# A decoder step on one core: every engine's order made by playing the program through with instruction durations

## The chip, the core and the metric

The kernel runs on one core of a Trainium2 chip, as one launch. The metric is the device time of that launch in microseconds; a lower time is better. A core has five engines that run side by side: TensorE (PE, matrix products), VectorE (DVE), ScalarE (ACT), GpSimd (POOL) and SyncE (SP, which here issues the DMAs). Each takes its instructions in the order in which the built program lists them, and a semaphore makes an instruction wait for what it needs from another engine.

## The reference

Two layers of a decoder trunk: an mLSTM mixer and a gated delta-net mixer, each followed by a squared-ReLU MLP, with a layer norm after every part. One sequence of 512 tokens starts from zero state, and eight sequences of 4 new tokens continue from stored states. D_MODEL is 1024, D_FF 4096; all is float32.

```python
def trunk(x, C, n, m, S, conv, ...):
    for layer in range(2):
        if layer % 2 == 0:
            y, Cj, nj, mj = mlstm_mixer(x, ...)        # 8 heads, key width 64, value width 128
        else:
            y, Sj, cj = gdn_mixer(x, ...)              # 16 value heads, 8 key heads, width 128
        x = layer_norm(ALPHA * x + y, ...)
        x = layer_norm(ALPHA * x + square(relu(x @ w1)) @ w2, ...)

def gated_delta_chunked(q, k, v, g, beta, S0):
    ...
    M = where(strict, (kb @ kc.T) * decay, 0)          # within a chunk
    A = M + eye(L)
    u, w = triangular_solve(A, [vc * beta, kb * exp(G)])
    attn = (qc @ kc.T) * decay
    def step(S, xc):                                   # from chunk to chunk
        v_new = u_c - w_c @ S
        o = qg_c @ S + attn_c @ v_new
        S = gL_c * S + kdec_c.T @ v_new
        return S, o
```

## The kernel before

All 544 tokens (512 of the prompt, 32 of the samples) lie side by side along the free dimension, in two halves of 272 columns; the features lie on the partitions in 8 blocks of 128. A projection's weight block is loaded by DMA (`wraw`, 512 KB), split into a high and a low part on ACT (L111) and DVE (L112), and multiplied in three products for each of 8 blocks and each half (`mm3`, L194). Such a 128 x 272 matmul of line 194 is the bulk of PE's work; the text calls it W. Both layers' MLPs are W almost alone.

The delta-net stage works in 8 units of two value heads (u = 0 to 7). The written order is a list:

```python
ORDER = "p0 p1 p2 p3 y0 w0 p4 p5 y1 w1 p6 p7 y2 w2 y3 w3"
PERIODS = {"p0": (3, 3, 4), "y0": (5, 5, 6), "p7": (3, 3, 6)}
```

`p` is the projections of a unit with the convolution (`conv`), `y` the output gate of a pair of units (`gate_out`), `w` the output projection. Each of them is 192 W. The small work runs in three lanes beside them, as generators that stop at each `yield`. After each group of three W, `mm3` calls `tick()`; a lane whose period is up then writes its next step into the program. `finish(...)` writes the rest of the named steps at once, as `gate_out` needs for the scans and the decode of its pair.

- Lane i, `prepare` and `invert`: products of the keys (L1093), decays (L1099, L1102), then a substitution of 15 steps on DVE (L1128, L1130) with DMAs through DRAM on both sides (`dg`, `ub`, `dx`, `xc`), then the inversion of eight triangular blocks in six groups of small matmuls: L1167 and L1174 (blocks of 32 x 16), L1188 and L1196/L1199 (32 x 32), L1208 and L1214 (64 x 64). Between two groups ACT or DVE copies the result.
- Lane s, `scan`: over 4 chunks of 128 tokens; in each chunk the products with the state (L1257), the solve with the inverse (L1268), the update of the state (L1275), the output (L1284), the head norm on ACT and DVE, and the transpose of the output (L1246, called the turn), which stands ahead of the next chunk's L1257.
- Lane d, `decode` and `update`: the sample tokens of a pair of units (L1315 to L1400), and their state updates (L1422) with loads and stores of `sst`.

The mLSTM stage has a list of its own (`ORDER_A`), with chunks of its scan on L742, L743, L757, L759, L762, and the transpose L735; its decode ends in L821, L824 and L834. Its scans and decodes are written with a raised priority (`high_priority(offset=HP)`), the loads of weights with `AHEAD`. A layer norm sums squares on PE (L356, L370) and sums on L367 and centres on L341.

All engines' final orders are made by the tile scheduler when `TileContext` is left: it takes the instructions by priority (the order in which they are written, less an offset) as their inputs and buffers come free. Buffers limit how far W can run ahead of the lanes: `kq` has 3 (`NKQ`), the PSUM tags have 3, 2, 2 and 1 (`BANKS`).

## Time and profile before

| what | us |
|---|---|
| median of 3 runs | 1823.6 |
| lowest, highest | 1813.73, 1825.53 |
| profiled execution, device time | 1814.86 |
| its span, first to last instruction | 1813.2 |
| PE busy | 1742.2 |
| DVE busy | 1062.3 |
| ACT busy | 831.2 |

The profiled execution lies near the lowest run. Busy times are unions over an engine's instructions. A PE row lasts until its modelled end, and rows overlap, so a step's cost on PE is read from the starts of rows that follow each other. The granted clock is 1.00 at PE's full 2.4 GHz and 0.50 at 1.2 GHz; in a window it is the mean.

### The profile page before, as it was taken

The page shows a single profiled execution, that of the slowest core. Times are in us where ns is not written, and L with a number is a line of the kernel's source. Part 1 is how long each engine was busy: PE and PEld are TensorE (multiplying, and loading weights), DVE is VectorE, ACT ScalarE, POOL GpSimd, SP SyncE. Part 2 cuts the span into 40 slices and gives each one's busy share as a digit, 9 for nine tenths or more (in the row PEclk, how much of TensorE's full clock was granted, in tenths as well). Part 3 has the DMA queues.
Part 4 walks back from the last instruction along what each step waited for, and adds up shares of the span by engine and source line. Part 5 has one row for each costly group of instructions (what it writes and reads, how often), then busy time and mean ns, then how long its engine had stood idle before and what let it go on. Part 6 is the DMA issues. An engine that isn't in the chain of part 4 may idle for free.

```text
span 1813.2 us, 35720 instructions
## 1 busy us (share of the span) xinstructions
PE 1742.2 (96%) x14580; PEld 1678.0 (93%) x14580; DVE 1062.3 (59%) x2648; ACT 831.2 (46%) x1874; POOL 56.1 (3%) x105
## 2 busy tenths in 40 slices
PE   7999999999999999899979999999898999999997
PEld 7999998999999999899869989998898999999996
DVE  6564767432244368777856877785488543234436
ACT  6444346331244137775644764575246542134314
POOL 2000000000000000011001000000000000000000
PEclk9999999999999999899979999997799999999998
DMA  4131232222223221223324323421242222222311
GB/s 161 59 106 62 70 97 93 71 94 82 94 82 117 82 75 62 56 58 102 104 64 143 105 66 104 141 80 39 78 132 73 94 85 91 90 86 93 106 59 50
DMA packets 84293, 158.89 MB, mean 88 GB/s; under 512 B 37536, under 2 KB 41504, under 8 KB 83616
## 3 DMA queue, kind: packets, MB, share of 16 engines
q1 hardware_dynamic: 84128, 156.60, 27.6%
q8 instruction: 115, 1.88, 0.4%
q14 instruction: 50, 0.41, 0.1%
HBM read 140.51 MB, written 16.06 MB: 86 GB/s over the span
## 4 chain that ended last, share of the span: by engine, by line
PE 80%; DVE 10%; ACT 4%; DMA 3%; issue 1%; POOL 1%; SPq 0%; ACTq 0%; DVEq 0%; POOLq 0%
PE pg_t L194 39%; PE pm_s L194 13%; PE pm_a L194 12%; PE pm_s L1371 2%; DVE lnt L380 1%; PE pm_s L1422 1%; DVE lnt L381 1%; PE pm_s L1257 1%; DMA xc<-dx 1%; PE pm_s L1268 1%; PE pm_a L1093 1%; DVE wl L112 1%; DVE acc L998 1%; PE pm_s L1275 1%; DVE XL L392 1%
## 5 line engine op out<-in xcount | busy, mean ns | idle before, releaser
L112 DVE TENSOR_TENSOR wl<-wraw,wh 128x1024 fp32r<-128x1024 f32 x200 | 245.3, 1227 | 370.6 <-ACT wh L111 369.8
L194 PE MATMUL pg_t<-XH,wh 128*128 128x272 f32 x1480 | 443.9, 300 | 3.3 <-ACT wh L111 2.8
L194 PE MATMUL pg_t<-XH,wl 128*128 128x272 f32 x1480 | 437.6, 296 | 1.0 <-DVE wl L112 1.0
L194 PE MATMUL pg_t<-XL,wh 128*128 128x272 f32 x1480 | 438.3, 296 | 0.0
L111 ACT CAST wh<-wraw 128x1024 fp32r<-128x1024 f32 (+1 forms) x201 | 210.1, 1045 | 472.7 <-PE pg_t L194 221.2
L194 PEld LDWEIGHTS pg_t<-XH,wh 128*128 128x128 f32 x1480 | 284.6, 192 | 7.4 <-ACT wh L111 4.5
L194 PEld LDWEIGHTS pg_t<-XH,wl 128*128 128x128 f32 x1480 | 283.8, 192 | 3.1 <-DVE wl L112 1.7
L194 PEld LDWEIGHTS pg_t<-XL,wh 128*128 128x128 f32 x1480 | 284.4, 192 | 2.0
L194 PE MATMUL pg_t<-h,wh 128*128 128x272 f32 x672 | 129.2, 289 | 0.0
L194 PEld LDWEIGHTS pg_t<-h,wh 128*128 128x128 f32 x672 | 105.8, 189 | 0.3
L194 PE MATMUL pg_t<-h,wl 128*128 128x272 f32 x336 | 97.0, 289 | 0.0
L194 PE MATMUL pm_a<-h,wh 128*128 128x272 f32 x496 | 95.3, 289 | 0.0
L194 PE MATMUL pm_s<-h,wh 128*128 128x272 f32 x496 | 95.0, 289 | 0.0
L194 PE MATMUL pm_s<-XH,wh 128*128 128x272 f32 x288 | 84.7, 294 | 0.0
L194 PE MATMUL pm_s<-XL,wh 128*128 128x272 f32 x288 | 84.4, 293 | 0.0
L194 PE MATMUL pm_s<-XH,wl 128*128 128x272 f32 x288 | 84.3, 293 | 0.0
L194 PE MATMUL pm_a<-XL,wh 128*128 128x272 f32 x280 | 82.3, 294 | 0.8 <-DVE XL L392 0.8
L396 DVE SCALAR_TENSOR_TENSOR XR<-XR,pg_t 128x272 f32<-128x272 f32 x118 | 51.0, 434 | 54.4 <-PE pg_t L194 53.9
L194 PE MATMUL pm_a<-XH,wh 128*128 128x272 f32 x280 | 82.6, 295 | 0.0
L194 PE MATMUL pm_a<-XH,wl 128*128 128x272 f32 x280 | 81.3, 290 | 0.0
L194 PEld LDWEIGHTS pm_s<-h,wh 128*128 128x128 f32 x496 | 78.0, 189 | 0.2
L194 PEld LDWEIGHTS pm_a<-h,wh 128*128 128x128 f32 x496 | 78.0, 188 | 0.1
(573 smaller groups left out, 3910.8 us busy)
## 6 DMA issues: line engine op xcount, KB each, us to landing
wraw<-in_w SPq DMA_DIRECT2D x64, 512.0 KB, 3.5
wraw<-in_wb SPq DMA_DIRECT2D x48, 512.0 KB, 3.5
wraw<-in_w2a SPq DMA_DIRECT2D x32, 512.0 KB, 3.5
sst<-in_s SPq DMA_DIRECT2D x64, 256.0 KB, 3.1
wraw<-in_wa SPq DMA_DIRECT2D x24, 512.0 KB, 3.5
wraw<-in_w2b SPq DMA_DIRECT2D x24, 512.0 KB, 3.5
wraw<-in_wbo SPq DMA_DIRECT2D x16, 512.0 KB, 3.7
out_ss<-sst SPq DMA_DIRECT2D x32, 256.0 KB, 2.7
```

Of the source, the lines that this page charges most:

```text
L111: S.copy(hi, src)
L112: V.tensor_tensor(lo, src, r32(hi), op=ALU.subtract)
L194: T.matmul(ps, lhsT=wt[:, k, :], rhs=xt[k][:, HS[h]], start=first and k == 0 and q == 0, stop=last and k == n - 1 and q == 2,)
L380: V.tensor_tensor(t, x, rs, op=ALU.mult)
L381: V.tensor_tensor(t, t, mu, op=ALU.subtract)
L392: V.tensor_tensor(XL[j][:, HS[h]], x, r32(XH[j][:, HS[h]]), op=ALU.subtract)
L396: V.scalar_tensor_tensor(x, x, ALPHA if first else 1.0, ps, op0=ALU.mult, op1=ALU.add)
L998: V.scalar_tensor_tensor(acc, pre[:, q:q + WC], cw[q], acc, op0=ALU.mult, op1=ALU.add)
L1093: T.matmul(pk[:, q * 256:(q + 1) * 256], lhsT=kq[:, 0, c0:c0 + P], rhs=kq[:, :, c0:c0 + P], start=True, stop=True)
L1257: T.matmul(pks[:, w], lhsT=kq[:, w, cc], rhs=St, start=True, stop=True)
L1268: T.matmul(pv[:, j], lhsT=X[:, 4 * (ch // 2) + 2 * j + ch % 2], rhs=rhs[:, j] if ch else vtok[:, j, 0], start=True, stop=True)
L1371: T.matmul(pkq[:, r], lhsT=t[:, r], rhs=kqf[:, :, o:o + 4], start=True, stop=True)
```

## The change

One keyword is given to the tile context. The scheduler then makes the orders by playing the program through with a duration for every instruction, from its own table, and gives an engine the next instruction at the time at which that play has it free. The kernel's functions, lists, buffers and priorities stay as they are.

```diff
-    with tile.TileContext(nc) as tc:
+    with tile.TileContext(nc, schedule_with_timeline_sim=True) as tc:
         hybrid_kernel(tc, *args)
```

Every engine's order changes: PE's by 9453 lines of difference, DVE's by 3606, ACT's, SP's and POOL's too. The number of instructions of each kind is the same on each engine. Three places on PE, before and after. In the names `pg_t`, `pm_a`, `pm_s` and `pm_t` are PSUM tiles, XH and XL the split activations, wh and wl the split weights.

The inversion of unit 0, lane i, at its fifth group, L1208, and the sixth, L1214. Before, 7 W stand between the two:

```order
L194 MATMUL pg_t<-XL_89,wh 128x272
L1208 MATMUL pm_a<-ZX,U 64x64 x8
L194 MATMUL pg_t<-XH_81,wl 128x272
L194 MATMUL pg_t<-XH_82,wh 128x272
L194 MATMUL pg_t<-XL_90,wh 128x272
L194 MATMUL pg_t<-XH_82,wl 128x272
L194 MATMUL pg_t<-XH_75,wh 128x272
L194 MATMUL pg_t<-XL_83,wh 128x272
L194 MATMUL pg_t<-XH_75,wl 128x272
L1214 MATMUL pm_a<-X,ZX 64x64 x8
```

After, the same place in PE's order; 25 W stand between L1208 and L1214, of which the first nine are shown:

```order
L194 MATMUL pg_t<-XL_83,wh 128x272
L194 MATMUL pg_t<-XH_75,wl 128x272
L1208 MATMUL pm_a<-ZX,U 64x64 x8
L194 MATMUL pg_t<-XH_76,wh 128x272
L194 MATMUL pg_t<-XL_84,wh 128x272
L194 MATMUL pg_t<-XH_76,wl 128x272
L194 MATMUL pg_t<-XH_77,wh 128x272
L194 MATMUL pg_t<-XL_85,wh 128x272
L194 MATMUL pg_t<-XH_77,wl 128x272
L194 MATMUL pg_t<-XH_78,wh 128x272
L194 MATMUL pg_t<-XL_86,wh 128x272
L194 MATMUL pg_t<-XH_78,wl 128x272
```

What moved: more W lie between two groups, and the whole inversion lies later against the W's, from the 5129th W to the 5163rd before and from the 5199th to the 5332nd after.

The scan of unit 0, lane s, from the turn (L1246) ahead of its second chunk, with steps of unit 1's preparation (L1093, L1099, L1102) and of the decode (L1315) between. Before:

```order
L1246 MATMUL pm_s<-ident,go_on 128x128 x2
L1257 MATMUL pm_s<-St,kq 128x256 x2
L1093 MATMUL pm_a<-kq 128x256
L1099 LDWEIGHTS identb
L1099 MATMUL pm_a<-maskw,identb 128x512
L1102 MATMUL pm_a<-RRb,hmr 128x256 x2
L194 MATMUL pg_t<-XL_83,wh 128x272
L194 MATMUL pg_t<-XH_75,wl 128x272
L194 MATMUL pg_t<-XH_76,wh 128x272
L194 MATMUL pg_t<-XL_84,wh 128x272
L194 MATMUL pg_t<-XH_76,wl 128x272
L1268 MATMUL pm_s<-rhs,X 128x128
```

After, the same steps:

```order
L1246 MATMUL pm_s<-ident,go_on 128x128 x2
L1257 MATMUL pm_s<-St,kq 128x256 x2
L1099 LDWEIGHTS identb
L1099 MATMUL pm_a<-maskw,identb 128x512
L1102 MATMUL pm_a<-RRb,hmr 128x256 x2
L1268 MATMUL pm_s<-rhs,X 128x128 x2
L1275 MATMUL pm_s<-vd,ktok 128x256
L1315 MATMUL pm_s<-blk,exprow 128x4
L1284 MATMUL pm_s<-vn,A 128x128 x2
L1323 MATMUL pm_s<-onesr,kqs 128x1 x2
L1246 MATMUL pm_s<-ident,go_on 128x128 x2
L1257 MATMUL pm_s<-St,kq 128x256 x2
```

What moved: W's no longer stand between the steps of a chunk; the next one comes after the L1268 of the fourth chunk.

The scan of unit 1, at the same point of its third chunk, with decode (L1400) and state updates (L1422) between. Before:

```order
L1246 MATMUL pm_s<-ident,go_on 128x128 x2
L1257 MATMUL pm_s<-St,kq 128x256 x2
L1400 MATMUL pm_s<-ident,onx 128x128
L1268 MATMUL pm_s<-rhs,X 128x128 x2
L1422 MATMUL pm_s<-VM,KM 128x512 x3
L194 MATMUL pg_t<-XH_75,wh 128x272
L1275 MATMUL pm_s<-vd,ktok 128x256
L194 MATMUL pg_t<-XL_83,wh 128x272
L194 MATMUL pg_t<-XH_75,wl 128x272
L194 MATMUL pg_t<-XH_76,wh 128x272
L194 MATMUL pg_t<-XL_84,wh 128x272
L194 MATMUL pg_t<-XH_76,wl 128x272
```

After, where the W's are those of the output projection (gyh is the gated output):

```order
L1246 MATMUL pm_s<-ident,go_on 128x128 x2
L1257 MATMUL pm_s<-St,kq 128x256 x2
L1400 MATMUL pm_s<-ident,onx 128x128
L1268 MATMUL pm_s<-rhs,X 128x128 x2
L1422 MATMUL pm_s<-VM,KM 128x512 x3
L194 MATMUL pg_t<-gyh,wh 128x272 x3
L1275 MATMUL pm_s<-vd,ktok 128x256
L1284 MATMUL pm_s<-vn,A 128x128 x2
L1422 MATMUL pm_s<-VM,KM 128x512 x3
L1246 MATMUL pm_s<-ident,go_on 128x128 x2
L1257 MATMUL pm_s<-St,kq 128x256 x2
L1422 MATMUL pm_s<-VM,KM 128x512 x3
```

What moved: the gate projection's W (XH, XL) stand ahead of this scan, and the scan runs into the inversion of unit 2 with three W in all.

## Rows read from the trace of the kernel before

**Rows 1.** The page's first part: span and PE's busy time
```profile
span 1813.2 us, 35720 instructions
...
PE 1742.2 (96%) x14580; PEld 1678.0 (93%) x14580; DVE 1062.3 (59%) x2648; ACT 831.2 (46%) x1874; POOL 56.1 (3%) x105
```

**Rows 2.** Busy time by stretches: PE, PEld, DVE, ACT, POOL, granted clock, DMA
```profile
50.00:250.00 200.00, 198.44 (x1543) 190.24 (x1542) 113.02 (x327) 87.02 (x274) 0.22 (x2) 1.00 0.24 78
250.00:320.00 70.00, 66.20 (x456) 61.34 (x455) 52.15 (x114) 43.27 (x82) 0.00 (x0) 0.95 0.29 91
350.00:650.00 300.00, 300.00 (x2389) 299.63 (x2388) 113.99 (x144) 85.41 (x123) 0.00 (x0) 1.00 0.28 90
650.00:1400.00 750.00, 709.36 (x6564) 666.09 (x6563) 553.51 (x1664) 433.28 (x1095) 43.27 (x74) 0.94 0.30 88
900.00:950.00 50.00, 40.42 (x425) 35.47 (x424) 28.23 (x93) 20.30 (x59) 3.54 (x8) 0.77 0.25 68
```

**Rows 3.** The chain that ended last, one piece in the first MLP
```profile
402.60 3.02 PE pg_t L194 x24
```

**Rows 4.** PE's timeline, inversion of unit 0, W left out: start, length, instruction
```profile
782.52 0.73 PE L1167 MATMUL pm_a<-DT,U 32*32 32x16 f32 x64 [0.76 <-DVE cvo L991]
...
784.40 0.73 PE L1174 MATMUL pm_a<-DB,Z 32*32 32x16 f32 x64
...
786.57 0.69 PE L1188 MATMUL pm_a<-DT,U 32*32 32x32 f32 x32
...
790.08 1.14 PE L1208 MATMUL pm_a<-ZX,U 64*64 64x64 f32 x16
...
792.22 1.14 PE L1214 MATMUL pm_a<-X,ZX 64*64 64x64 f32 x16
```

**Rows 5.** W alone in two stretches: PE, PEld, granted clock, DMA
```profile
782.50:793.50 11.00, 6.13 (x34) 4.62 (x34) 1.00 0.18 55
911.90:923.80 11.90, 0.82 (x2) 0.50 (x2) 0.50 0.16 56
```

**Rows 6.** PE's timeline, inversion of unit 2, first and last group
```profile
911.99 1.05 PE L1167 MATMUL pm_a<-DT,U 32*32 32x16 f32 x64 [4.31 <-DVE DT L1159]
...
921.80 1.97 PE L1214 MATMUL pm_a<-X,ZX 64*64 64x64 f32 x16 [0.68 <-ACT ZX L1210]
```

**Rows 7.** PE's timeline, two waiting steps of scans 1 and 6
```profile
882.79 0.71 PE L1268 MATMUL pm_s<-rhs,X 128*128 128x128 f32 x4 [0.94 <-ACT osm L1402]
...
1280.92 0.41 PE L1246 MATMUL pm_s<-ident,go_on 128*128 128x128 f32 x2 [3.05 <-DVE xb L1130]
```

**Rows 8.** Timeline, unit 6: last decay product, first group of its inversion
```profile
1200.86 0.59 PE L1102 MATMUL pm_a<-RRb,hmr 128*128 128x256 f32 x2
...
1231.11 1.05 PE L1167 MATMUL pm_a<-DT,U 32*32 32x16 f32 x64 [0.71 <-DVE DT L1159]
```

**Rows 9.** PE's timeline, steps that wait for a convolution
```profile
727.24 1.10 PE L1093 MATMUL pm_a<-kq 128*128 128x256 f32 x4 [2.07 <-DVE kq L1002]
...
756.44 1.12 PE L1040 MATMUL pm_t<-ident,kq 128*128 128x128 f32 x4 [3.33 <-DVE kq L1002]
```

**Rows 10.** PE's timeline, mLSTM scan: end of a chunk's output, its transpose
```profile
197.40 0.39 PE L759 MATMUL pm_s<-cnp,qs 128*128 128x129 f32 x2
...
200.41 0.41 PE L735 MATMUL pm_s<-ident,ho_hn 128*128 128x128 f32 x2
```

**Rows 11.** PE's timeline, waits around three layer norms
```profile
281.48 0.73 PE L356 MATMUL pm_t<-lnt,onesr 128*128 128x272 f32 x2 [1.17 <-ACT lnt L352]
...
684.24 0.72 PE L356 MATMUL pm_t<-lnt,onesr 128*128 128x272 f32 x2 [1.46 <-ACT lnt L352]
...
1398.77 0.39 PE L194 MATMUL pg_t<-gyh,wh 128*128 128x272 f32 x1 [1.71 <-DVE XR L396]
```

**Rows 12.** DMA issues by line: KB each, median us from issue to landing
```profile
wraw<-in_wb SPq DMA_DIRECT2D x48, 512.0 KB, 3.5
```

## The prediction

> **What bounds the kernel now.** I read the page first, then the busy time of each engine by stretches, then the timeline of TensorE (PE) where it stops. PE is busy for 1742.2 of 1813.2 us [rows 1], so the kernel is bound by PE, and only PE's own stops and slow stretches can be given back. The windows show where they lie [rows 2]. In the first MLP, 350 to 650 us, PE is busy all the time. In the mLSTM stage, 50 to 250 us, it is idle for 1.6 us. Around the end of that layer, 250 to 320 us, it is idle for 3.8 us. In the delta-net stage, 650 to 1400 us, it is idle for 750 - 709.36 = 40.6 us, with a granted clock of 0.94. The worst stretch there is 900 to 950 us, with 9.6 us idle and a granted clock of 0.77.
>
> Idle time understates the stops. The chain shows 24 projection matmuls in 3.02 us, so one takes 0.126 us of PE [rows 3], while its row is 0.29 us long: about 0.16 us of every wait is covered by the row before it. I therefore reckon in starts of rows. A bare step, one with no projection matmuls between a lane's step and the step that needs its result, costs PE the whole way through VectorE (DVE) or ScalarE (ACT) and back. I call the 10752 projection matmuls of line 194 W below.
>
> No instruction is added or removed: both orders have 12960 matmuls, 490 DMAs on SP, the same count of every operation on every engine, and two ACT table loads. PE's order goes from 397 runs of W to 300. So there is nothing to price but waits, and each is priced by how many W (0.126 us each) stand in PE's order between a step and what it needs, before and now.
>
> **The change part by part.**
>
> *Inversions that get cover.* Unit 0's inversion runs from 782.52 to 793.36 us, 10.8 us [rows 4], with 34 W inside [rows 5], 4.3 us. Its own six groups, each about 0.25 us shorter than its row because rows overlap (the sixth, L1196 with L1199, taken as long as L1208), come to 0.5 + 0.5 + 0.4 + 0.9 + 0.9 + 0.9 = 4.1 us, and a transpose on L1040 to 0.4. That leaves 2.0 us of waiting. In before, the eight inversions hold 34, 36, 2, 13, 32, 29, 26 and 37 W; in after 133, 81, 0, 118, 3, 128, 25 and 51. Five (units 0, 1, 3, 5, 7) then have at least 51, and I take their waits to be gone: 5 x 2 = **-10 us** (0 to -13).
>
> *Inversions that lose it.* Unit 2's inversion is the nearest row for a bare one: 911.99 to 923.77 us, 11.8 us [rows 6], with 2 W and at half clock [rows 5]. Twice 4.1 us is own work, so some 3.5 us are waits. Unit 4 goes from 32 W to 3, and unit 6 loses the cover of its second half: **+3 us** for both (2 at full clock; 10 if at half clock).
>
> *Scan 0 and the substitution of unit 1.* In before 160 W lie in scan 0; in after its first three chunks have none (second order piece of the change section). A bare chunk waits on PE three times. The turn waited 3.05 us for the normalised head at 1280.92, and the solve waited 0.94 us after the products with the state at 882.79 [rows 7]; I take the step from the solve to the state update as another 0.9. That makes 4.9 us, three times 14.7, less 4.5 us for preparation and decode matmuls that stand between: 10. In the same place the chain from the last decay product of unit 1 (L1102) to its inversion has only 18 W left instead of 214. That chain took 30.2 us from 1200.86 to 1231.11 for unit 6 [rows 8]. On DVE only 9 other operations now stand in it instead of 45, so I take 24 us; scan 0 covers about 19.5 of them and leaves some 5 us. Less some 2 us that the place costs now: **+13 us** (6 to 22).
>
> *Scan 1 and inversion 2.* Two bare chunks, 9.8 us, less six groups of state updates (L1422) of 0.7 us between them: 6; the substitution of unit 2 keeps 37 W of 105: 5. The same place now holds 4.3 us of idle time ahead of the inversion at 911.99 [rows 6] and some 6 us in shorter waits: **+1 us** (-5 to +8).
>
> *Scan 7.* It keeps 28 W of 201, at the end of the last gate projection, and nothing is left behind it but the output projection that needs it. Four turns, three solves and four updates, less the state updates between, come to 13 us, and 3 us from the last turn to the first W that needs it. The place now loses some 5 us: **+11 us** (5 to 16).
>
> *Steps that gain cover.* Products and transposes behind a convolution waited 2.07 us at 727.24 and 3.33 at 756.44 [rows 9], and two more about as long later. The first (L1093 of unit 0) now has 72 W ahead that it did not have. The others stand behind the same W as before, or behind fewer, and should wait as they do: **-2 us** (0 to -8). Scans 2 to 6 go from 95 to 256 W to 227 to 332: **-8 us** for their short waits, an estimate from the 40.6 us of idle time less what is named here. The end of the third gate projection (3.05 us idle at 1280.92 [rows 7], and a shorter one) gets some 24 W at every step: **-4 us**.
>
> *mLSTM stage.* One place becomes bare: two chunks of scan 1 and the first part of decode 0 stand without W. In before the head's way from L759 at 197.40 to its transpose at 200.41 takes 3.0 us [rows 10], with 1.2 us of matmuls in it; two chunks, the last turn and some 5 us of decode steps come to 10. The other steps go from 4 to 12 W to 13 to 28, which can give back no more than the small waits behind the 1.6 us of idle time, an estimate of 6: **+4 us** (-4 to +10).
>
> *Layer norms.* The sums of the second half waited 1.17 us at 281.48, 1.46 at 684.24, and a W waited 1.71 at 1398.77 [rows 11]. In after the next layer's W and the gate products stand between these sums: **-7 us** of the three places' 5 us of such waits and shorter ones (-2 to -10).
>
> *The clock.* In 650 to 1400 us a granted clock of 0.94 means 12% of the time at 1.2 GHz in place of 2.4. The slow parts follow PE's stops, as behind the 4.3 us at 911.99. After loses stops at the inversions and at 1280 us and gains them in scans 0, 1 and 7: **0 us** (-15 to +15).
>
> *Weight loads.* A weight load lands 3.5 us after its issue [rows 12], and the loads still stand ahead of PE's need. On SP, loads of unit 3's stage now stand behind the substitution's DMAs of unit 1, which wait; the W that need them are themselves behind that wait on PE. Nothing, as long as that holds; if it doesn't, one load of 3.5 us in each of a few places.
>
> Sum: -10 + 3 + 13 + 1 + 11 - 2 - 8 - 4 + 4 - 7 + 0 = **+1 us**. The profiled execution took 1814.9 us, so 1816; it is 8.7 us under the median of the runs shown, 1823.6, whose runs lie 11.8 us apart. For the median I forecast 1823.6 + 1, **1825 us**: no change that can be measured, taking 1% (18 us) as about what a measurement of this kernel can tell.
>
> **The rivals.**
>
> *Faster: bare chains are cheap.* With W's gone, DVE and ACT have no evictions or weight splits between the lane's steps, so a bare chunk may wait 2.5 us, not 4.9, and the substitutions hide behind the scans. Then the bare costs 3 + 15 + 11 + 16 + 10 = 55, reckoned before what those places lose now, halve to 27; the places lose 2 + 10 + 5 = 17 now, and the savings elsewhere are 10 + 2 + 8 + 4 + 6 + 7 = 37. With 10 of the clock's loss given back that is 27 - 17 - 37 - 10 = -37, so **1787 us**. For it: DVE is busy 553.5 of 750 us in that stage [rows 2], so its queue is what the lanes wait in. Against it: the 3.05 us at 1280.92 were bare as well.
>
> *Slower: the bare stretches fall to the half clock.* One mechanism, in four places: scan 0 with inversion 1, scan 1 with inversion 2, inversion 4, scan 7. The stretch 900 to 950 us is such a place now: 9.6 us idle, and (1 - 0.77) x 50 = 11.5 us of full-speed time lost [rows 2], 21 us. Four of them cost 84 us in place of the one there is now; with 37 us saved elsewhere and 10 added in the mLSTM stage that is +57 as it stands, +36 with the old one counted off: **1860 us** by the lower. It decides once a bare stretch holds stops like the 4.3 us ahead of 911.99 [rows 6], behind which the inversion ran at half clock [rows 5]. The page "TensorE: Matmul & The Clock Gate" of the Trainium skill, section "HAM oscillation — how this bites in real kernels", has this rule: PE that sits idle between bursts is throttled again, and each burst starts slow. By that rule every one of the four places pays; the half clock behind 911.99 agrees for the one bare place that this trace has.
>
> That the order hardly moves is excluded: the two orders differ on every engine, and the counts above are far apart.
>
> **How the numbers follow.** I give the forecast 0.38, the faster rival 0.33, the slower one 0.29. Both signs hold most of the chance, so the likeliest case's own range is 1806 to 1842. The range to hold 8 in 10 takes in most of both rivals: **1780 to 1864 us**. Faster by over 1% 0.33, within 1% 0.37, slower by over 1% 0.30; the forecast's tails are split between the outer two.
>
> **What would show it.** In the profile after: inversions 0, 1, 3, 5 and 7 with no idle row on PE inside; a bare scan 0 with turns that wait about 3 us; PE idle of 15 to 20 us between the preparation of unit 1 and its inversion; scan 7's last turns waiting at the end of the stage; no wait ahead of unit 0's first L1093. If bare turns wait 1.5 us or less, the faster rival holds; if the granted clock of the stage falls under 0.92, the slower one. I am wrong altogether if the first MLP stretch changes, which has no idle time to give, or if PE waits long for W's weights, whose loads I priced at nothing.

## The result, and the profile after

The changed kernel takes 1928.4 us (median of 4 runs, 1922.1 to 1931.3) against 1818.9 for the kernel before: a ratio of 1.0595, 95% interval [1.0544, 1.0646]. It is 110 us slower; 1825 was forecast, with a range to 1864. The first part of the page after, which answers to [rows 1]:

```profile
span 1920.3 us, 35689 instructions
...
PE 1789.1 (93%) x14580; PEld 1716.8 (89%) x14580; DVE 1069.1 (56%) x2648; ACT 829.8 (43%) x1874; POOL 59.6 (3%) x105
```

PE does the same work. Its idle time grew by 60 us, from 1813.2 - 1742.2 = 71 us to 1920.3 - 1789.1 = 131, and the same instructions kept it busy 47 us longer. The mean granted clock fell from 0.971 to 0.943, which is 2 x (0.057 x 1920 - 0.029 x 1813) = 114 us more spent at half clock. The busy time by stretches shows where, with the columns of [rows 2]; the stages lie later, so the stretches are longer:

```profile
50.00:250.00 200.00, 190.39 (x1440) 184.91 (x1440) 103.06 (x299) 81.58 (x262) 0.22 (x2) 0.96 0.21 68
250.00:345.00 95.00, 79.72 (x502) 74.58 (x502) 61.98 (x143) 46.89 (x94) 0.00 (x0) 0.84 0.23 78
350.00:700.00 350.00, 350.00 (x2789) 349.84 (x2788) 136.77 (x174) 105.27 (x154) 0.78 (x2) 1.00 0.28 90
700.00:1500.00 800.00, 725.04 (x6458) 669.98 (x6456) 547.99 (x1651) 422.85 (x1082) 44.02 (x72) 0.91 0.27 81
850.00:890.00 40.00, 30.06 (x177) 25.07 (x175) 24.25 (x90) 16.98 (x55) 1.24 (x2) 0.80 0.14 34
945.00:1000.00 55.00, 42.03 (x377) 32.26 (x376) 35.74 (x127) 23.73 (x72) 4.67 (x9) 0.75 0.31 95
```

The MLP is as full as before. The mLSTM stage now idles for 9.6 us (1.6 before), the end of that layer for 15.3 (3.8), the delta-net stage for 75 (40.6). The two short stretches are the bare scans 0 and 1. PE's timeline in scan 0, whose three chunks stand without W (start, length, instruction, idle time ahead and releaser):

```profile
867.53 0.68 PE L1268 MATMUL pm_s<-rhs,X 128*128 128x128 f32 x4 [0.53 <-DVE rhs L1260]
869.25 0.70 PE L1275 MATMUL pm_s<-vd,ktok 128*128 128x256 f32 x2 [1.04 <-DVE vd L1270]
870.74 1.19 PE L1284 MATMUL pm_s<-vn,A 128*128 128x128 f32 x4 [0.67 <-DVE scolb L1317]
875.09 0.66 PE L1246 MATMUL pm_s<-ident,go_on 128*128 128x128 f32 x2 [2.51 <-DVE xb L1130]
875.54 1.91 PE L1257 MATMUL pm_s<-St,kq 128*128 128x256 f32 x4
877.99 1.19 PE L1268 MATMUL pm_s<-rhs,X 128*128 128x128 f32 x4 [0.54 <-DVE rhs L1260]
...
885.92 0.41 PE L1246 MATMUL pm_s<-ident,go_on 128*128 128x128 f32 x2 [2.29 <-DVE go_on L1233]
```

A chunk waits at the turn, the solve and the update, as the prediction had it. The L1268 takes 0.68 us at 867.53 and 1.19 at 877.99: between the two the clock went to one half. The mLSTM stage has the same behind its 552nd W, where decode 0 and two chunks stand bare:

```profile
120.08 0.33 PE L735 MATMUL pm_s<-ident,ho_hn 128*128 128x128 f32 x1 [2.20 <-DVE ho_hn L722]
...
123.20 5.15 PE L821 MATMUL pm_s<-cn,QX 128*128 128x129 f32 x32
130.62 0.33 PE L824 MATMUL pm_s<-ident,ho_hn 128*128 128x128 f32 x1 [2.27 <-DVE ho_hn L722]
```

Inversions with cover lose no time in stops, but they became long: those of units 0, 1, 3, 5 and 7 take 24.2, 29.2, 30.6, 29.0 and 27.7 us from the first group to the last, against 10.0 to 12.2 before. Unit 0 shows why. First ACT's timeline at the copy that the sixth group needs, then PE's at that group, then the W's between the two (columns: PE, PEld, clock, DMA):

```profile
852.02 0.59 ACT L1210 ACTIVATE ZX<-pm_a 64x512 f32<-64x512 f32 x1 [0.73 <-PE pm_a L1208]
```

```profile
855.24 0.33 PE L1214 MATMUL pm_a<-X,ZX 64*64 64x64 f32 x2
```

```profile
852.62:855.24 2.62, 2.62 (x22) 2.47 (x20) 1.00 0.00 0
```

The copy ended at 852.61 and the group started 2.63 us later, behind some 20 W that PE took while the operand lay ready. Before, the copy ended at 791.85 and the group followed 0.37 us later:

```profile
791.26 0.59 ACT L1210 ACTIVATE ZX<-pm_a 64x512 f32<-64x512 f32 x1 [0.65 <-PE pm_a L1208]
```

Read in the same way, the five covered inversions let 10.6 to 15.2 us pass over their five handovers (from the end of a group's copy to the start of the next group), 0.7 to 1.9 before. The mLSTM's transpose L735 comes at a median of 2.45 us after its operand, 0.15 before. In the inversions a covered step mostly starts 15 to 25 matmuls after its operand is ready, before none to four.

The layer norms grew. From the first half's L370 to the second half's last L356 they take 16.2, 16.6, 16.2 and 16.1 us before and 24.4, 21.7, 29.8 and 18.3 after. The first ends with this wait for the split activations of the next layer:

```profile
328.92 0.59 PE L194 MATMUL pm_a<-XH,wh 128*128 128x272 f32 x1 [4.58 <-ACT XH L391]
```

### The profile page after: what moved, and what is told of

Read it like the earlier page. It is cut to its first block, busy times and chain, and to the rows that moved or that the text cites. A ratio compares the mean times of both kernels' runs of the same rounds, so it can differ in the third digit from the quotient of the medians.

```text
span 1920.3 us, 35689 instructions
## 1 busy us (share of the span) xinstructions
PE 1789.1 (93%) x14580; PEld 1716.8 (89%) x14580; DVE 1069.1 (56%) x2648; ACT 829.8 (43%) x1874; POOL 59.6 (3%) x105
## 4 chain that ended last, share of the span: by engine, by line
PE 80%; DVE 11%; ACT 5%; DMA 2%; issue 2%; SPq 0%; POOL 0%; ACTq 0%; DVEq 0%; POOLq 0%
PE pg_t L194 39%; PE pm_s L194 12%; PE pm_a L194 12%; PE pm_s L1371 2%; PE pm_s L1422 1%; PE pm_s L1257 1%; DVE wl L112 1%; DVE XR L396 1%; PE pm_a L1093 1%; PE pm_t L356 1%; DVE sst L1427 1%; PE pm_s L1268 1%; PE pm_s L1284 1%; DVE lnt L380 1%; DVE acc L998 1%
## 5 line engine op out<-in xcount | busy, mean ns | idle before, releaser
L194 PEld LDWEIGHTS pg_t<-XH,wh 128*128 128x128 f32 x1480 | 288.4, 195 | 13.2 <-ACT wh L111 5.1
L396 DVE SCALAR_TENSOR_TENSOR XR<-XR,pg_t 128x272 f32<-128x272 f32 x118 | 50.7, 433 | 55.7 <-PE pg_t L194 55.4
L998 DVE SCALAR_TENSOR_TENSOR acc<-pre,cst,acc 128x568 f32<-128x568 f32 x96 | 77.3, 807 | 2.5 <-ACT acc L996 1.6
```

The lines of the kernel that those rows point to most:

```text
L194: T.matmul(ps, lhsT=wt[:, k, :], rhs=xt[k][:, HS[h]], start=first and k == 0 and q == 0, stop=last and k == n - 1 and q == 2,)
L396: V.scalar_tensor_tensor(x, x, ALPHA if first else 1.0, ps, op0=ALU.mult, op1=ALU.add)
L998: V.scalar_tensor_tensor(acc, pre[:, q:q + WC], cw[q], acc, op0=ALU.mult, op1=ALU.add)
```

## The experiments

Ten of the sixteen runs hold the order of some engines. The helper adds an order edge from each instruction of an engine to the next in a table; such an edge sets the place in that engine's queue and makes no semaphore wait. The tables are the orders of the built kernels before and after; in two runs DVE's is put together from two builds.

```diff
         hybrid_kernel(tc, *args)
+        in_order(tc, nc, TABLES)
...
+def in_order(tc, nc, tables):
...
+        for a, b in zip(order, order[1:]):
+            tc.add_manual_dep(byname[b], byname[a].name, mybir.DependencyInfo(
+                mybir.DependencyClass.NoSync, mybir.DependencyReason.DATA), reason="in_order")
```

**PE's order alone.** The first theory was the prediction's own: the loss lies in PE's order (theory A). The rival put it in DVE's and ACT's (theory B).

> The changed kernel, with PE's instructions held in the order that they had before (by order edges alone, which add no wait between engines); DVE, ACT, POOL and SP get their orders from the play. Theory A, PE's order carries the loss: the bare runs of lane steps are gone, so the time is within 15 us of before, some 1820 to 1835 us. Theory B, the orders of DVE and ACT carry it (evictions, weight splits and layer-norm steps queued behind lane steps): most of the 110 us stays, 1890 us or more. Both alike: about 1875.

> The mirror image: the kernel before, its scheduler without the play, with PE's instructions held in the order of the changed kernel; the other engines' orders follow from the scheduler of before. Theory A: about the changed kernel's time, 1905 to 1930 us. Theory B: under 1860.

Measured: 1929.6 us, ratio 1.060 [1.055, 1.065], with PE as before; 1998.7 us, 1.099 [1.095, 1.102], with PE as after. Theory A fell on the first: PE has its old order, W for W, and the time did not come back. It is not the same loss, though: the stretches of over 8 us between the starts of two W come to 33 us before, 195 in the changed kernel and 73 in this run. Two lines of its list of waits, PE's alone (us in total, times, longest):

```profile
PE pm_t L356 <- ACT lnt L352: 20.9, 9, 5.3
PE pm_a L1167 <- DVE DT L1159: 16.8, 3, 7.5
```

The norm's sums and the inversions wait for operands that DVE and ACT deliver late. The second run refutes the simple theory B too, which gave it under 1860; it is slower than either theory has it. PE's order from one scheduler does badly beside the orders that the other gives DVE and ACT, both ways round.

> The kernel before, PE in the changed kernel's order from the start to the first MLP (the mLSTM stage and its layer norm), in the order of before from there on. By the ends of the stages in the two traces this part holds +37 us of the +107 of the spans: Theory A: 1850 to 1858. Theory B: within 10 us of before.

> The kernel before, PE in the changed kernel's order in the delta-net stage and its layer norm alone. By the ends of the stages this part holds +66 us: Theory A: 1880 to 1892, and with the run of the mLSTM part the two losses add up to that of the whole order within 10 us. Theory B: under 1840.

Measured: 1861.6 us, 1.024 [1.019, 1.028], and 1959.8 us, 1.077 [1.073, 1.081]; the second lies far outside both ranges. The parts add up, 42 + 140 = 182 against 179 for the whole, but the delta-net part costs twice what that stage lost in the changed kernel. Forced beside the other scheduler's DVE and ACT, PE's order is worse than with its own companions.

**Which engines belong together.**

> The changed kernel with the orders of PE, DVE and ACT all three held as they were before; SP (the DMA issues) and POOL keep the play's. Theory C, the orders of the three engines belong together and the loss is in them: 1812 to 1832 us. Theory S, the play's order of the loads on SP carries a part that neither single-engine run could take away: 1850 or more.

> The changed kernel with the orders of DVE and ACT held as before, PE's made by the play around them. It has 30 stretches of five or more different lane steps on PE with no W between, before and after have 14 each. Theory D, the orders of DVE and ACT carry the loss and PE's follows from them: 1815 to 1840 us. Theory C: PE's play is off by itself: 1870 to 1930.

Measured: 1822.9 us, 1.0003 [0.998, 1.003], with three engines held; 2025.3 us, 1.111 [1.106, 1.115], with DVE and ACT held and PE free. Theory C holds in the first: the whole loss is in the orders of PE, DVE and ACT taken together, and the play's order of DMA issues and POOL costs nothing. In the second, theory D falls, and PE's order by the play, made around the old orders of the other two, costs twice what C allowed.

> The changed kernel with the orders of PE and DVE held as before, ACT's, SP's and POOL's from the play. With PE alone held the time was 1930 us, with PE, DVE and ACT held 1823. Theory V, DVE's order (the fullest engine beside PE, 553 of 750 us in the delta-net stage before) carries what is left: 1820 to 1840 us. Theory X, ACT's order carries it: 1890 or more. A part each: about 1860.

> The mirror image: the orders of PE and ACT held as before, DVE's from the play. Theory V: 1890 to 1930 us, and the layer norms stay long (24 us from the sums of the first half to those of the second, 16 before). Theory X: 1820 to 1845.

Measured: 1854.8 us, 1.014 [1.010, 1.018], with ACT free; 1916.2 us, 1.049 [1.045, 1.052], with DVE free. With PE in its old order, DVE's order by the play costs 93 us and ACT's 32 (both together 110, in the first run): mostly theory V, with a part for ACT.

> PE and ACT in the orders of before; DVE in the order of before but for the four layer norms, where it has the order that the play made in the run with PE and ACT held (268 places of 2648 differ). That run took 93 us more than before, and its four layer norms, from the sums of the first half to the last sums of squares of the second, took 90 us in place of 65. Theory N, the norms' part of DVE's order costs this by itself: 1843 to 1855 us. Rival, the norms are long there because what comes ahead of them is late: within 10 us of before.

> The same with DVE's order from the play in the delta-net stage alone, between its layer norms (1037 places differ). In the run with DVE free the stage took 59 us more than before without its norm. Theory N: 1870 to 1890 us, and with the run of the norms and some 10 us of the mLSTM stage the parts add up to 93. If the parts need each other: under 1850.

Measured: 1844.4 us, 1.012 [1.009, 1.016], and 1887.5 us, 1.036 [1.032, 1.039]. Both hit: 24 us for the norms, 67 for the delta-net stage, together 91 of the 93. The norms show how an order of DVE does it. DVE's timeline before, in the first layer norm: from 276.0 to 280.9 us the first half's chain L380, L381, L392 has no step of the second half in it.

```profile
278.11 0.44 DVE L392 TENSOR_TENSOR XL<-XR,XH 128x272 fp32r<-128x272 f32 x1
278.46 0.44 DVE L381 TENSOR_TENSOR lnt<-lnt,lnb 128x272 f32<-128x272 f32 x1
278.81 0.44 DVE L380 TENSOR_TENSOR lnt<-XR,lnb 128x272 f32<-128x272 f32 x1
```

The same place in the run with the play's order in the norms alone, DVE and then PE:

```profile
278.31 0.43 DVE L381 TENSOR_TENSOR lnt<-lnt,lnb 128x272 f32<-128x272 f32 x1
278.66 0.43 DVE L396 SCALAR_TENSOR_TENSOR XR<-XR,pm_s 128x272 f32<-128x272 f32 x1
279.01 0.78 DVE L381 TENSOR_TENSOR lnt<-lnt,lnb 128x272 f32<-128x272 f32 x2
279.71 0.43 DVE L360 TENSOR_TENSOR lnb<-lnb,XR 128x272 f32<-128x272 f32 x1
280.06 0.43 DVE L396 SCALAR_TENSOR_TENSOR XR<-XR,pg_t 128x272 f32<-128x272 f32 x1
280.41 0.43 DVE L396 SCALAR_TENSOR_TENSOR XR<-XR,pm_a 128x272 f32<-128x272 f32 x1
```

```profile
289.75 4.42 PE L356 MATMUL pm_t<-lnt,onesr 128*128 128x272 f32 x8 [6.44 <-ACT lnt L352]
```

Steps of the second half (L396, L360), ready early and needed late, stand between those of the first, so the chain ends at 291 us in place of 283. ACT, whose queue is in the old order, has the second half's squares (L352) behind the first half's chain, and PE waits 6.44 us for them, then works at a granted clock of 0.50: eight L356 take 4.42 us, 2.97 in the same place before, a wait of 0.60 included.

**Written places and more W.** Two runs of the changed kernel with other lists, and two of the kernel before.

```diff
-PERIODS = {"p0": (3, 3, 4), "y0": (5, 5, 6), "p7": (3, 3, 6)}
+PERIODS = {"p0": (1, 1, 2), "y0": (2, 2, 3), "p7": (1, 1, 2)}
```

> The changed kernel with the lanes written about twice as densely (periods 1, 1, 2 and 2, 2, 3 in place of 3, 3, 4 and 5, 5, 6). Four of the eight inversions still hold over 75 W as played. Theory L, the play holds a lane's results back longer than the chip does, whatever the written places: the time stays within 25 us of the changed kernel's 1928, and the covered inversions still have operands that lie ready 10 us or more before PE takes them. Theory W, the written places set the cover: denser lanes finish the scans ahead of the output projections, 1850 to 1885.

```diff
-ORDER = "p0 p1 p2 p3 y0 w0 p4 p5 y1 w1 p6 p7 y2 w2 y3 w3"
+ORDER = "p0 p1 p2 p3 y0 p4 w0 p5 y1 p6 w1 p7 y2 w2 y3 w3"
```

> The changed kernel with w0 written behind p4 and w1 behind p6, so that 192 W that need no scan stand ahead of the first two output projections. Theory A, the W ran out ahead of the projections that need the scans: the bare stretches at W 5568 and W 6354 go and with them 25 to 45 us, 1885 to 1905. Rival: the play spends the added W elsewhere and other stretches become bare: 1915 to 1940.

Measured: 1954.4 us, 1.072 [1.067, 1.077], with denser lanes, and 1918.1 us, 1.052 [1.046, 1.057], with later output projections. Theory W is out: denser lanes are slower by 26 us, one more than theory L's bound, and the inversions of units 3, 5 and 7 still let 13.0 to 13.5 us pass over their handovers, while unit 0's lost its cover altogether. Later projections brought 10 us of the 25 to 45 expected: the W were spent elsewhere, as the rival had it. The bare stretches around W 6354 shrank, but the inversion of unit 6, with 25 W inside in the changed kernel, now lies in 40 us without any (W alone, with the columns of [rows 5]):

```profile
1303.80:1343.50 39.70, 0.00 (x0) 0.00 (x0) 0.70 0.09 23
```

> The kernel before, its scheduler without the play, with w0 written behind p4 and w1 behind p6, as in the run of the changed kernel with that list. If the bare place at the inversion of unit 2 (900 to 950 us, 21 us lost) is for want of W that need no scan, it goes: 1800 to 1812 us. If the list only shifts the bare place: 1815 to 1830.

```diff
-ORDER = "p0 p1 p2 p3 y0 w0 p4 p5 y1 w1 p6 p7 y2 w2 y3 w3"
+ORDER = "p0 p1 p2 p3 p4 y0 w0 p5 p6 y1 w1 p7 y2 w2 y3 w3"
```

> The kernel before with p4 written ahead of y0 and p6 ahead of y1: 192 W more stand ahead of the first two gates and their scans. Same two readings: 1800 to 1812 us if W that need no scan were wanting there, 1815 to 1830 if not.

Measured: 1815.5 us, 0.994 [0.991, 0.998], and 1808.6 us, 0.991 [0.988, 0.994]. The first falls, by half a us, in the second reading, and its trace agrees: unit 2's inversion has 28 W, 2 before, but unit 3's now has none. The second falls in the first reading: W that need no scan were wanting there, and with them it is faster than both kernels of this case, a little. Its inversion of unit 2, last below, has 34 W at a clock of 0.96, in place of 2 at 0.50 [rows 5]. W alone in units 2 and 3 of the first run and in unit 2 of the second:

```profile
911.00:926.40 15.40, 6.16 (x28) 4.86 (x28) 0.74 0.14 47
987.50:1001.90 14.40, 0.00 (x0) 0.00 (x0) 0.50 0.16 46
...
913.20:924.30 11.10, 5.72 (x35) 4.51 (x34) 0.96 0.20 58
```

**A count or a time?** The last question was why a covered step stands behind so many W in the play's order.

```diff
+                for c in range(2 if lanes else 1):
+                    cs = slice(136 * c, 136 * c + 136) if lanes else slice(0, HN)
...
-                    rhs=xt[k][:, HS[h]],
+                        rhs=xt[k][:, HS[h]][:, cs],
```

> The changed kernel with each W of the delta-net stage's lanes cut into two matmuls of 136 columns (same work, twice the instructions). In the changed kernel a covered lane step stands behind 17 to 21 matmuls that PE takes after the step's operand is ready, about 2.5 us. Theory Q, the play hands PE a fixed count of instructions ahead of their execution: still 14 to 22 matmuls, now halves, and 1.2 to 1.7 us; the play costs less against its own twin without the play than 110 us (50 to 85). Theory L2, the play holds results back by a fixed time: 34 to 42 halves, still 2.5 us; 100 us or more against the twin.

> The twin: the kernel before, its scheduler without the play, with the W of the delta-net stage's lanes cut into two. It tells what the cut itself costs. If a half takes half the time on PE: within 15 us of before; if a weight load bounds it, up to 300 us more.

Measured: 2260.8 us, 1.237 [1.229, 1.245], with the play; 2613.4 us, 1.433 [1.424, 1.442], without. Covered steps of the inversions still stand mostly behind 15 to 22 matmuls, now halves, which is theory Q's count, but at full clock 2.0 to 2.6 us after their operands, which is near theory L2's time. Neither falls, because the pair doesn't separate them: a half took 0.111 us from start to start at full clock, nearly as long as the whole W's 0.126. Why the play leaves that gap stays open, and with halves it is not the play's alone: in the twin without the play the groups of all eight inversions start 13 to 38 halves after their operands are ready, where the kernel before had none to four W. The twin's time missed both of its readings: 793 us more than before, where 5856 halves in place of 2928 W come to 5856 x 0.111 - 2928 x 0.126 = 281 us at full clock. The play's price can't be read against it.

## Why the prediction was wrong

To follow it by its own steps, I took for each PE row in both traces the distance to the next start, less what that kind of row takes at full clock in before (the 30th percentile of its distances); what a row at half clock takes more, up to double, counts as clock, the rest as wait. Cut at the same W in both orders, after less before ("inversions 0, 1" are those of units 0 and 1, and so on):

| step (W from, to) | forecast | waits | half clock |
|---|---|---|---|
| mLSTM stage (0 to 1460) | +4 | +9.0 | +9.2 |
| layer norms | -7 | +13.6 | +8.7 |
| convolution waits (4848 to 4996) | -2 | +7.1 | -1.9 |
| inversions 0, 1, scan 0, substitution 1 (4996 to 5500) | -4 + 13 | +8.0 | +6.5 |
| scan 1, inversion 2 (5500 to 5600) | +1 | +3.0 | +3.4 |
| inversions 4 and 6, bare (6340 to 6358, 7104 to 7110) | +3 | +17.2 | +10.2 |
| inversions 3, 5, 7, scans 2 to 6, third gate's end | -18 | -14.0 | -1.6 |
| scan 7 (7480 to 7607) | +11 | +14.6 | +7.8 |
| the clock | 0 | | (42.3 in all) |

The columns sum to +58.5 and +42.3, 101 of the 107 us between the spans.

**The step that failed first** is "So there is nothing to price but waits, and each is priced by how many W (0.126 us each) stand in PE's order between a step and what it needs, before and now." It read one engine's order where three had changed. With PE's order put back alone the kernel was still 110 us slower; with DVE's and ACT's put back as well, it was not slower at all. By size the 100 us that the forecast lacks are the clock, set at nothing (42.3), the norms' waits (20.6), those of inversions 4 and 6 (14.2) and of the convolutions (9.1); the rest is smaller. Where W cover was really the limit it sized well: scan 0 with its neighbours (+9 forecast, +8.0), scan 7 (+11, +14.6), the saved waits of the covered places (-18, -14.0). Where DVE's queue sets the chain it had even the sign wrong: the norms (-7, +13.6) and the steps behind a convolution (-2, +7.1). Of those the first lost its wait as forecast, but the transpose waited 5.30 us, 3.33 before [rows 9]:

```profile
779.89 1.13 PE L1093 MATMUL pm_a<-kq 128*128 128x256 f32 x4 [0.23 <-DVE colpb L964]
...
799.09 1.12 PE L1040 MATMUL pm_t<-ident,kq 128*128 128x128 f32 x4 [5.30 <-DVE kq L1002]
```

I had credited the norms with the W that now stand between their sums, and not looked at how the two halves' steps stand on DVE. That the play's DVE order lengthens the norms by itself, beside the old orders of PE and ACT, is shown; for the convolutions it is argued from the same pattern.

**The mLSTM stage** and **the bare inversions 4 and 6** were right in mechanism and too small. The mLSTM's bare place alone took +12.6 us of waits, where the step had 10 and then set 6 against it. The inversions were priced as an inversion alone; each stands in one bare run with steps of a scan and of the next unit's preparation, which wait as well. A piece of each, all engines with the columns of [rows 2]:

```profile
1152.00:1164.40 12.40, 10.07 (x252) 8.56 (x250) 5.19 (x17) 7.09 (x25) 3.30 (x7) 0.84 0.06 21
...
1327.60:1348.80 21.20, 15.96 (x152) 13.25 (x152) 9.23 (x20) 12.16 (x32) 2.85 (x6) 0.68 0.10 29
```

**The clock** was set at 0 on the ground that lost stops and new ones cancel. They don't: the new bare places of the delta-net stage brought 3 to 6 us of it each, and only around the third gate's end some 12 us came back. The slower rival had this mechanism and four of the places. By its rule from the page "TensorE: Matmul & The Clock Gate" of the Trainium skill, section "HAM oscillation — how this bites in real kernels", PE that idles between bursts is throttled anew; the trace agrees at scan 0, where L1268 goes from 0.68 to 1.19 us. The rival priced a place at 21 us, which counts idle time at half clock twice; scan 0's came to 13.0 + 4.7 and scan 7's to 13.2 + 6.3. Its 1860 was short by the norms, the mLSTM stage and the convolutions, which no rival held.

**The faster rival** expected bare turns of 1.5 us or less; they waited 1.8 to 2.5 us in scans 0 and 7, with one of 4.0 in scan 1. **The signs named** came as said for inversions 0, 1, 3, 5 and 7, scan 0 and scan 7, nearly so for unit 0's first L1093 (0.23 us), and the stage's clock fell under 0.92 (0.91). PE's idle rows between the preparation of unit 1 and its inversion came to 8.7 us, not to 15 to 20. The two that were to show it wrong altogether did not: the MLP is unchanged and the weights are in time.

That the loss lies in the three orders together is shown. How they make it is what I hold: they have lane steps 15 to 25 W later on PE than their operands allow on this chip, and steps that are ready early ahead of urgent ones on DVE; so lanes run long, and W that need no scan are used up before the output projections, where the scans then stand bare and the clock falls. The late steps, the bare places and the DVE part of it are in rows and runs. How the 110 us of the changed kernel divide among its engines can't be told, since no engine's order stood well without its companions, and why the play spaces steps so stays open.

## What to carry to other kernels

When a scheduler's whole output changes, price it on every engine that a chain passes through: an order of PE that reads better in cover says little without the order that DVE got beside it. Holding the order of one engine, then two, then three with order edges finds in a few runs where such a loss sits; a single engine's result says little, as the 1930 and 1999 us of PE's two orders show. And a place without cover costs twice, once in waits and once in the clock behind them, here some 13 and 5 to 6 us for scans 0 and 7.

## What the runs showed of the hardware

Matmuls with half the columns cost almost the whole. With 136 columns they start 0.111 us apart at full clock, against 0.126 for 272, and 0.213 us apart at half clock, against 0.227. PE stayed at half clock without a stop: in the run with the play, 80 us of the delta-net stage have PE busy for all 80 at a clock of 0.50, while W of 272 columns run at 1.00 under the same full load [rows 2].

```profile
1400.00:1480.00 80.00, 80.00 (x373) 77.89 (x373) 18.56 (x46) 12.40 (x31) 0.00 (x0) 0.50 0.16 53
```

The clock had fallen at 1391 us, with PE busy for all of the 20 us from 1380 to 1400. So idle time is not all that lowers the clock here. The twin without the play had a mean clock of 0.64 in that stage, the run with it 0.79, which is where most of the 350 us between them lie; why their clocks differ was not tried.
